# Choosing the gathered tokens first and the first tokens last in a two-block transformer kernel's expert layer

## The chip, the cores and the metric

The kernel runs on one core of one Trainium2 chip. The metric is the device time of one execution in microseconds (us). TensorE (PE in the rows) multiplies matrices, VectorE (DVE) and ScalarE (ACT) work element by element, GpSimd (POOL) does small element work here and issues the indirect DMAs, and SyncE (SP) issues most other DMAs. PEld is TensorE's loading of weights, which overlaps its matmuls.

## The reference

The program computes a first transformer block of two layers and then a second block; the change concerns only the end of the second block, a layer of 16,384 small experts for 512 tokens of 1024 values. Cut to that:

```python
def chunk_fn(hc):                                   # 128 tokens
    q = (hc @ w_query).reshape(128, 8, 256)         # 8 heads
    s1 = einsum('chk,nk->chn', q[..., :128], keys_1)
    s2 = einsum('chk,nk->chn', q[..., 128:], keys_2)
    v1, i1 = top_k(s1, 16)
    v2, i2 = top_k(s2, 16)
    cand = v1[..., :, None] + v2[..., None, :]      # 256 candidates per head
    top_s, pos = top_k(cand, 16)
    experts = take_along_axis(i1 * 128 + i2, pos)   # 16 experts per head
    gate = softmax(top_s)
    act = gelu(einsum('chkd,cd->chk', expert_u[experts], hc))
    return einsum('chk,chkd->cd', gate * act, expert_v[experts])
```

So each token has 8 x 16 = 128 chosen experts, each with a row of `expert_u` and a row of `expert_v` (1024 values each) and a gate.

## The kernel before

**Two ways for the experts.** The first 368 tokens (`TD`) are done densely: every expert's `u` is multiplied with all 368 tokens, GELU is taken, the result is multiplied with a gate that is zero where the expert was not chosen, and `v` is multiplied in. The last 144 tokens (`GTOK`) are gathered: for each of 144 columns one indirect DMA of 0.5 MB (`rows`, L1387) fetches one expert row for each of 128 tokens, VectorE multiplies it with the tokens' activations and sums (L1398), and after 144 rows of `u` come 144 rows of `v` (L1408). One such fetch with the vector instruction that belongs to it is called a gathered step here; there are 288, and step i works on the row that was fetched three steps earlier (`LAG`). Five `rows` tiles are there (`NROW`).

**fp32 by three products.** Each weight tile `raw` (1 MB) is split into a high part `whi` (ScalarE) and the rest `wlo` (VectorE), both at L242, and each product is three matmuls (`mm3`, L276 to L278). In the dense part a matmul has 368 columns. A unit is 1 MB of weights: two halves of 24 matmuls, 48 in all.

**The routing stage.** `w_query` gives the queries (matmuls of 512 columns), and for each head and chunk of 128 tokens `select(c, h)` takes the two top-16 lists and the top 16 of their sums on VectorE (L1170 to L1190, candidates added on GpSimd). `choose(c)` turns them into gates and row and column numbers of the experts (L1196 to L1236). `matrices(c)` transposes these on TensorE (L1263) and builds the gates of a dense chunk in slices of 16 tokens: for two steps per slice VectorE makes one-hot tiles `ob` (L1302) and `oa` (L1307, two of them), TensorE multiplies them (L1316, 32 matmuls of 128 columns in fp16 per slice), ScalarE copies the result (L1319) into `stage`, and a DMA puts it into DRAM (`gd`). Chunks 0, 1 and 2 have 8, 8 and 7 slices. Chunk 3 is gathered, as are the last 16 tokens of chunk 2.

**Order of the work.** `fill(n)` puts dense `u` units into this stage (12 in all, their results are written to DRAM as `spilled` and read back later by `back`); then come 8 more `up` units, and then the loop over 16 groups of 8 expert columns: the gates' tile `gt` (a DMA on ScalarE's queue, L1452), multiplication of `a` with it (L1464), a split of the product, 192 matmuls with `v`, and further `up` units. `pace()` advances the gathered steps evenly over this loop. A scheduler at build time puts each engine's instructions into one fixed order, with priorities given by `tc.high_priority`; it may put work of a later line ahead of an earlier one if tiles are free. Each engine then runs its own order strictly. A tile pool's memory goes to the next pool only after the pool is closed: `right` holds the routing stage's tiles `gm` and closes after the last `matrices`, and `er`, which comes after, takes the same memory.

In the kernel before, the chunks are chosen in the order 0, 1, 2, and 3 after `right.close()`; the tiles `a` that take the GELU results of all `u` units are in the pool `pp`, which is open from the start.

Of the kernel before, what the change touches and what calls it, by code (L numbers as in the profile page):

```python
# [21 lines left out]
P = 128  # L22
# [36 lines left out]
HNU = 4  # L59
# [10 lines left out]
OBB = 3  # L70
# [125 lines left out]
def block_kernel(ctx, tc, x_in, cs_in, wst, vec, cst, gmask, smask, pos, ada1, ada2, wgate, keys, ust, uex, vst, vex, out):  # L196
# [910 lines left out]
    with tc.tile_pool(name="peer", bufs=1, reuse_waits="tile") as pp:  # L1107
# [18 lines left out]
        def up(j2, eng=None, spill=None):  # L1126
            u = unit(ust[j2], eng=eng)
            for jj in range(2):
                p = bank("mm")
                for k in range(KD):  # L1130
                    o = (jj * KD + k) * P
                    mm3(p[:, :TD], *part(u, o, P), hh[k][:, :TD], hl[k][:, :TD],
                        k == 0, k == KD - 1)
                a = pp.tile([P, TD], F32, tag="a", bufs=NA, name="a")
                A_.activation(a, p[:, :TD], AF.Gelu_apprx_tanh)
                acts[2 * j2 + jj] = a
                if spill is not None:
                    SP.dma_start(spilled[spill + jj], a)

        def back(j2, spill):  # L1140
            for jj in range(2):
                a = pp.tile([P, TD], F32, tag="a", bufs=NA, name="a")
                SP.dma_start(a, spilled[spill + jj])
                acts[2 * j2 + jj] = a

        with tc.tile_pool(name="sel", bufs=1, reuse_waits="tile") as sp:
            cho = {}
# [100 lines left out]
            def matrices(c):  # L1248

                res = choose(c)  # L1250
                fill(FILL[c])
# [33 lines left out]
                for s in range(c0 // TS, min(c0 + P, TD) // TS):  # L1285
# [12 lines left out]
                    for q0 in range(0, 4, TQ):  # L1298
# [6 lines left out]
                        for i in range(2):  # L1305
                            o = gm.tile([P, TQ, P, 4], F16, tag=f"oa{i}", bufs=OBB, name="oa")
                            V.tensor_mul(  # L1307
# [4 lines left out]
                        for q in range(TQ):  # L1312
                            p = bank("acc")
                            for t in range(4):
                                for i in range(2):
# [6 lines left out]
                                 st.rearrange("p (g j) t -> p g j t", j=JG))  # L1322


            late = []
            for h in range(PH):
                qq, ql = [], []
                for half in range(2):
                    p = proj("w_query_2", hh, hl)
                    t = sp.tile([P, 3 * P], F32, tag="q", bufs=4, name="q")  # L1330
                    A_.copy(t, p[:, :S - P])
                    l = sp.tile([P, P], F32, name=f"ql{h}_{half}")
                    A_.copy(l, p[:, S - P:])
                    qq.append(t)
                    ql.append(l)
# [11 lines left out]
            if GTOK:  # L1347
                res = choose(NT - 1)
                V.tensor_copy(gates, res[0])
                V.scalar_tensor_tensor(eidx, res[1], 128.0, res[2], op0=ALU.mult, op1=ALU.add)  # L1350
            else:
                matrices(NT - 1)
# [6 lines left out]
        with tc.tile_pool(name="exp", bufs=1, reuse_waits="tile") as ep:  # L1359
            def gathered():  # L1360

                hn, hx = [er.tile([P, D], F32, name=f"hn{i}") for i in range(2)]
                with tc.high_priority(2 * AHEAD), tc.issue_after(mark.ins):
                    for e, tk in enumerate((slice(S - P, S), slice(TD, S - P))):
                        for k in range(KD):
                            if k % 4 == 0:
                                p = bank("acc")
                            t = er.tile([P, P], F32, tag="hs", bufs=2, name="hs")
                            if e:
                                V.tensor_add(t.rearrange("p (t q) -> p t q", q=EQ),  # L1370
                                             hh[k][:, tk, None].bitcast(F32).to_broadcast([P, EX, EQ]),
                                             hl[k][:, tk, None].bitcast(F32).to_broadcast([P, EX, EQ]))
                            else:
                                V.tensor_add(t, hh[k][:, tk].bitcast(F32), hl[k][:, tk].bitcast(F32))
                            T_.transpose(p[:, (k % 4) * P:(k % 4 + 1) * P], t, ident)
                            if k % 4 == 3:
                                A_.copy((hx if e else hn)[:, (k - 3) * P:(k + 1) * P], p)
                y, yx = [ep.tile([P, D], F32, name=f"y{i}") for i in range(2)]
                act = ep.tile([P, P + EX], F32, name="act")
                sel = ep.tile([P, EX], F32, name="sel")  # L1380
                V.reduce_sum(sel, ident.rearrange("p (t q) -> p t q", q=EQ), axis=mybir.AxisListType.X)
                rows = []
                for i in range(2 * (P + EX) + LAG):
                    if i < 2 * (P + EX):
                        n = i % (P + EX)
                        r = ep.tile([P, D], F32, tag="rows", bufs=NROW, name="rows")
                        G_.indirect_dma_start(out=r, out_offset=None, in_=uex if i < P + EX else vex,  # L1387
                                              in_offset=bass.IndirectOffsetOnAxis(
                                                  ap=eidx[:, n:n + 1] if n < P else eidx2[:, n - P:n - P + 1], axis=0))
                        rows.append(r)  # L1390
                    if i < LAG:
                        yield
                        continue
                    r = rows.pop(0)
                    n = (i - LAG) % (P + EX)
                    up_ = i - LAG < P + EX
                    if up_:
                        V.scalar_tensor_tensor(r, r, 1.0, hn if n < P else hx, op0=ALU.mult, op1=ALU.mult,  # L1398
                                               accum_out=act[:, n:n + 1])
                        if n == P + EX - 1:  # L1400
                            A_.activation(act, act, AF.Gelu_apprx_tanh)
                            V.tensor_mul(act[:, :P], act[:, :P], gates)
                            V.tensor_mul(act[:, P:], act[:, P:], gates2)
                    elif n in (0, P):
                        V.tensor_scalar(yx if n else y, r, act[:, n:n + 1], None, op0=ALU.mult)
                    else:
                        z = y if n < P else yx
                        V.scalar_tensor_tensor(z, r, act[:, n:n + 1], z, op0=ALU.mult, op1=ALU.add)  # L1408
                    yield
                for k in range(KD):  # L1410
                    if k % 4 == 0:
                        p = bank("mm")
                    T_.transpose(p[:, (k % 4) * P:(k % 4 + 1) * P], y[:, k * P:(k + 1) * P], ident)
# [165 lines left out]
```

## Time and profile before

| | |
|---|---|
| median of three runs | 2811.03 us (2804.39 to 2818.14) |
| the profiled execution's own time | 2807.13 us |
| its span, first to last instruction | 2805.4 us |
| TensorE busy | 2699.4 us, 96% |
| VectorE busy | 2095.0 us, 75% |
| matmuls | 14889 |
| mean granted TensorE clock | 0.988 of full |

A busy time adds the stretches in which an engine had an instruction in work; TensorE's matmuls overlap, so the time that one takes from its neighbours is read from the distance between two starts and not from the duration. The profile's line of slices cuts the span into 40 equal pieces of 70.1 us.

### The profile page before, as it was taken

Reading aid. Unit: us, or ns where it says so; the run is one execution under the profiler, and the core shown is the slowest. Engines: PE = TensorE matmul, PEld = TensorE weight load, DVE = VectorE, ACT = ScalarE, POOL = GpSimd, SP = SyncE. Lnnn points to the kernel's source line nnn. Section 1 sums busy time; section 2 is a strip of 40 time slices with the busy share of each in tenths; the row PEclk is TensorE's granted clock in tenths of the full one; section 3 lists DMA queues with packets and bytes.
Section 4 is the critical chain, followed back from the end, with each engine's and each line's share of the span. In section 5 each row is a group of like instructions: output and inputs, shape, how many; then the busy total and the mean of one; then the engine's idle time right before and its main releaser. Section 6 shows DMA issues by size and latency. Waiting matters only on the chain.

```text
span 2805.4 us, 38971 instructions
## 1 busy us (share of the span) xinstructions
PE 2699.4 (96%) x14889; PEld 2438.1 (87%) x14889; DVE 2095.0 (75%) x4028; ACT 1059.9 (38%) x1530; POOL 741.4 (26%) x638
## 2 busy tenths in 40 slices
PE   6789999999999999999999999999999999999998
PEld 4677888888788888888888789998999999999998
DVE  8874755556786654558866897789987988888996
ACT  4443422223443322233543246653333333333332
POOL 4631000000010100001511500004544545555550
PEclk9899999999999999999999999999999999999998
DMA  6441355553212555522222237667999998999983
GB/s 262 145 143 61 124 192 195 173 204 108 76 46 83 197 186 180 173 90 92 100 81 93 80 126 230 201 197 281 355 334 353 334 349 324 345 333 341 338 333 140
DMA packets 159788, 560.62 MB, mean 200 GB/s; under 512 B 13248, under 2 KB 66912, under 8 KB 124912
## 3 DMA queue, kind: packets, MB, share of 16 engines
q1 hardware_dynamic: 101648, 332.62, 33.7%
q0 software_dynamic: 55296, 201.35, 20.1%
q10 hardware_dynamic: 2656, 24.15, 2.2%
q8 instruction: 117, 1.92, 0.3%
q14 instruction: 71, 0.58, 0.1%
HBM read 527.32 MB, written 30.75 MB: 199 GB/s over the span
## 4 chain that ended last, share of the span: by engine, by line
PE 60%; DVE 14%; issue 12%; POOL 8%; DMA 5%; ACT 1%; POOLq 0%; SPq 0%; DVEq 0%; ACTq 0%
PE mm L277 15%; PE mm L276 15%; PE mm L278 15%; POOL rows L1387 7%; PE acc L1316 3%; DMA rows<-vex,eidx 3%; DVE wlo L242 3%; PE acc L278 2%; PE acc L277 2%; PE acc L276 2%; PE acc L646 1%; DMA rows<-uex,eidx 1%; PE acc L365 1%; DVE aw L481 1%; PE acc L935 1%
## 5 line engine op out<-in xcount | busy, mean ns | idle before, releaser
L242 ACT CAST whi<-raw 128x1024 fp32r<-128x1024 f32 x510 | 532.4, 1051 | 1304.3 <-PE mm L277 691.9
L277 PE MATMUL mm<-hl,whi 128*128 128x512 f32 (+2 forms) x2544 | 899.8, 354 | 4.0 <-DVE hl L429 3.1
L278 PE MATMUL mm<-hh,wlo 128*128 128x512 f32 (+2 forms) x2544 | 899.2, 354 | 3.6 <-DVE wlo L242 3.6
L276 PE MATMUL mm<-hh,whi 128*128 128x512 f32 (+2 forms) x2544 | 897.6, 354 | 4.2 <-ACT hh L428 3.2
L242 DVE TENSOR_TENSOR wlo<-raw,whi 128x1024 fp32r<-128x1024 f32 x488 | 598.9, 1231 | 234.6 <-ACT whi L242 223.6
L277 PEld LDWEIGHTS mm<-hl,whi 128*128 128x128 f32 x2544 | 482.3, 190 | 52.1 <-DVE hl L429 4.4
L278 PEld LDWEIGHTS mm<-hh,wlo 128*128 128x128 f32 x2544 | 482.7, 190 | 51.0 <-DVE wlo L242 4.4
L276 PEld LDWEIGHTS mm<-hh,whi 128*128 128x128 f32 x2544 | 481.1, 190 | 51.2 <-ACT hh L428 3.8
L1387 POOL DMA_INDIRECT rows<-vex,eidx x144 | 233.0, 1618 | 193.8 <-DVE y L1408 176.4
L1387 POOL DMA_INDIRECT rows<-uex,eidx x144 | 214.6, 1490 | 211.3 <-DVE rows L1398 165.8
L322 POOL DMA_DIRECT2D araw<-ada x96 | 51.0, 531 | 657.3 <-DVE araw L315 625.9
L1408 DVE SCALAR_TENSOR_TENSOR y<-rows,act,y 128x1024 f32<-128x1024 f32 x142 | 181.8, 1281 | 46.4 <-DMA rows<-vex,eidx 45.4
L1398 DVE SCALAR_TENSOR_TENSOR rows<-rows,hn 128x1024 f32<-128x1024 f32 x144 | 172.1, 1223 | 47.1 <-DMA rows<-uex,eidx 47.0
L315 DVE SCALAR_TENSOR_TENSOR araw<-araw,sc 128x1024 f32<-128x1024 f32 x128 | 158.1, 1258 | 8.7 <-DMA araw<-ada 8.7
L277 PE MATMUL mm<-fl,whi 128*128 128x512 f32 (+1 forms) x396 | 144.9, 366 | 0.0
L278 PE MATMUL mm<-fh,wlo 128*128 128x512 f32 (+1 forms) x396 | 144.9, 366 | 0.0
L276 PE MATMUL mm<-fh,whi 128*128 128x512 f32 (+1 forms) x396 | 144.7, 365 | 0.0
L743 DVE TENSOR_TENSOR s<-s,mm 128x512 f32<-128x512 f32 x42 | 28.9, 688 | 129.9 <-PE mm L278 129.4
L1319 ACT ACTIVATE stage<-acc 128x512 f32<-128x512 f32 x92 | 91.7, 1106 | 36.9 <-PE acc L1316 26.6
L451 DVE SCALAR_TENSOR_TENSOR x<-mm,mod,x 128x512 f32<-128x512 f32 (+1 forms) x66 | 44.1, 668 | 82.2 <-PE mm L278 82.1
L1316 PE MATMUL acc<-oa,ob 128*128 128x128 f16 x736 | 101.5, 296 | 0.3 <-DVE oa L1307 0.2
L1316 PEld LDWEIGHTS <-ob 128*128 128x128 f16 x736 | 76.8, 118 | 13.5 <-DVE oa L1307 0.6
(1383 smaller groups left out, 4659.9 us busy)
## 6 DMA issues: line engine op xcount, KB each, us to landing
raw<-wst SPq DMA_DIRECT2D x127, 1024.0 KB, 4.9
raw<-ust SPq DMA_DIRECT2D x64, 1024.0 KB, 7.1
raw<-vst SPq DMA_DIRECT2D x64, 1024.0 KB, 7.5
araw<-ada POOLq DMA_DIRECT2D x96, 512.0 KB, 4.5
gd<-stage SPq DMA_DIRECT2D x23, 1024.0 KB, 4.5
gt<-gd ACTq DMA_DIRECT2D x16, 1472.0 KB, 12.0
araw<-ada SPq DMA_DIRECT2D x32, 512.0 KB, 4.4
aw<-ada SPq DMA_DIRECT2D x16, 512.0 KB, 8.4
```

Of the source, the lines that this page charges most:

```text
L242: state["split"] = (A_.copy(hi, src), (eng or V).tensor_sub(lo, src, hi.bitcast(F32)))
L276: T_.matmul(out_, wh, ah, start=first, stop=False)
L277: T_.matmul(out_, wh, al, start=False, stop=False)
L278: state["mm"] = T_.matmul(out_, wl, ah, start=False, stop=last)
L315: op(out=w, in0=w, scalar=1.0, in1=sc, op0=ALU.mult, op1=ALU.mult, accum_out=out_)
L322: (G_ if l else SP).dma_start(raw, w[n * P:(n + 1) * P, :])
L451: return V.scalar_tensor_tensor(x[n][:, cs], p[:, cs], gate[:, n:n + 1], x[n][:, cs], op0=ALU.mult, op1=ALU.add)
L1316: T_.matmul(p[:, t * P:(t + 1) * P], ob[:, q, :, t], oa[i][:, q, :, t], start=i == 0, stop=i == 1)
L1319: A_.mul(st[:, :, t1:t1 + 4].rearrange("p j t -> p t j"), p.rearrange("p (t j) -> p t j", t=4), 1.0 / GSC)
L1387: G_.indirect_dma_start(out=r, out_offset=None, in_=uex if i < P + EX else vex, in_offset=bass.IndirectOffsetOnAxis(ap=eidx[:, n:n + 1] if ...
L1398: V.scalar_tensor_tensor(r, r, 1.0, hn if n < P else hx, op0=ALU.mult, op1=ALU.mult, accum_out=act[:, n:n + 1])
L1408: V.scalar_tensor_tensor(z, r, act[:, n:n + 1], z, op0=ALU.mult, op1=ALU.add)
```

## The change

The order of chunks in the routing stage is reversed. Chunk 3 is chosen first, right after the queries, and its gathered steps begin there: three at once, one after each slice of gates, and two after each of the eight `up` units. Then come `matrices(2)`, four heads of chunk 0's `select`, `matrices(1)`, the other four heads, and `matrices(0)`. The queries of chunk 0 are kept in the two tiles that later take `y` and `yx`. The tiles of the gathered part move to a pool `ga` that is open from before the routing stage. The tiles `a` are now a function `tile_a`: four of them in the routing stage's pool `sel`, for the units that are spilled, and after `right.close()` sixteen in `er`, in the memory that `gm` had. `ob` and `oa` have two buffers each where they had three (`OBB`). The first `gt` is allocated and loaded after the split weights' first tiles. Line numbers after the change are one lower up to L1102 and up to 72 and 19 higher behind (L1316 becomes L1388, L1398 becomes L1187, L1464 becomes L1483, L276 to L278 become L275 to L277).

```diff
-OBB = 3
+OBB = 2
...
+        ga = gs.enter_context(tc.tile_pool(name="ga", bufs=1, reuse_waits="tile"))
+        hn, hx = [ga.tile([P, D], F32, name=f"hn{i}") for i in range(2)]
+
+        def rows_tile():
+            return ga.tile([P, D], F32, tag="rows", bufs=NROW, name="rows")
...
+            def tile_a():
+                return sp.tile([P, TD], F32, tag="a", bufs=4, name="a")
...
-                a = pp.tile([P, TD], F32, tag="a", bufs=NA, name="a")
+                a = tile_a()
...
-                fill(FILL[c])
+                fill(FILL[NT - 2 - c])
...
                     SP.dma_start(gd[:, :, s, :, :].rearrange("g p j t -> p g j t"),
                                  st.rearrange("p (g j) t -> p g j t", j=JG))
+                    some(oh.ins)
...
-                for c in range(NT - 1):
-                    cs = slice(c * P, (c + 1) * P)
+                for c in (3, 2, 1):
+                    cs = slice((c - 1) * P, c * P)
                     select(c, h, qq[0][:, cs], qq[1][:, cs])
-                late.append(ql)
-            for c in range(NT - 1):
-                matrices(c)
+            res = choose(NT - 1)
+            V.tensor_copy(gates, res[0])
+            V.scalar_tensor_tensor(eidx, res[1], 128.0, res[2], op0=ALU.mult, op1=ALU.add)
+            side["g"] = gathered()
+            step(LAG)
+            done = [LAG]
+
+            def some(ins, n=1):
+                with tc.issue_after(ins):
+                    step(n)
+                done[0] += n
+
+            def late_select(hs):
+                for h in hs:
+                    select(0, h, late[0][:, h, :], late[1][:, h, :])
+
+            matrices(2)
+            late_select(range(0, 4))
+            matrices(1)
+            late_select(range(4, 8))
+            matrices(0)
             G_.memset(gm.tile([P, 120], F32, name="end"), 0.0)
             right.close()
-            er = ctx.enter_context(tc.tile_pool(name="er", bufs=1, side="right", reuse_waits="tile"))
-            for h in range(PH):
-                select(NT - 1, h, late[h][0], late[h][1])
...
             fill(NSP)
-            for j2 in range(NA // 2):
-                up(j2, eng=V)
-                if j2 == HNU:
-                    mark = state["mm"]
...
+        er = ctx.enter_context(tc.tile_pool(name="er", bufs=1, side="right", reuse_waits="tile"))
+
+        def tile_a():
+            return er.tile([P, TD], F32, tag="a", bufs=NA, name="a")
+
+        for j2 in range(NA // 2):
+            up(j2, eng=V)
+            some(state["split"][1].ins, 2)
...
-            per = (2.0 * (P + EX) + LAG - FIRST) / (todo - LAST)
-            step(FIRST)
+            per = (2.0 * (P + EX) + LAG - done[0]) / (todo - LAST)
...
-            gt = gate_load(0)
             for g in range(P // GJ):
...
+                    if j == 0:
+                        gt = gate_load(0)
```

The body of `gathered()` is the same but for its pool and for `y`, which is allocated at the first `v` row.

The order in which the instructions stand shows where the work went. First TensorE, at the place where the last dense chunk's gates begin. Before, this is chunk 2: the last gate matmuls (`acc<-oa,ob`) of chunk 1, one transpose of the gates `g`, and behind it matmuls of dense units (`mm<-hh,whi` and the like, 40 up to the next transpose).

```order
L1316 LDWEIGHTS ob
L1316 MATMUL acc<-oa,ob 128x128
L1263 MATMUL acc<-ct,g 128x128
L277 MATMUL mm<-hl_105,whi 128x368
L278 MATMUL mm<-hh_97,wlo 128x368
L276 MATMUL mm<-hh_98,whi 128x368
```

So the transposes had dense matmuls before and behind them. After the change the last dense chunk is chunk 0. Its place on TensorE reads as follows (`acc<-ky,ql` are the products of `select` for chunk 0).

```order
L1388 LDWEIGHTS ob
L1388 MATMUL acc<-oa,ob 128x128
L1237 MATMUL acc<-ky,ql 128x128 x5
L1335 MATMUL acc<-ct,g 128x128
L1335 MATMUL acc<-ct,e 128x128 x2
L1388 LDWEIGHTS ob
L1388 MATMUL acc<-oa,ob 128x128
```

No dense matmul stands there any more. In the order before, dense matmuls stand between the gate matmuls of every step of all three chunks. In the order after, 672 dense matmuls (14 units) stand ahead of chunk 1's first gate matmul, none between there and the last gate matmul of chunk 0 (512 gate matmuls), and 288 (6 units) in one block behind it.

The second place is VectorE where the gates are done and the dense groups begin. Before, the choosing of chunk 3 (`po`, `g`, `du`) stands between the multiplications with the gates' tile (`a<-a,gt`) and the splits:

```order
L1190 MAX_INDEX po<-top,w_15342 128x8
L242 TENSOR_TENSOR wlo<-raw,whi 128x1024
L1196 TENSOR_TENSOR g<-top 128x128
L1209 TENSOR_SCALAR du<-po 128x128 x2
L1464 TENSOR_TENSOR a<-a,gt 128x368 x3
L242 TENSOR_TENSOR wl__16336<-a,wh__16335 128x368
```

After, the last one-hot tiles of chunk 0 are followed by nine gathered steps, and then by the next split:

```order
L1374 TENSOR_TENSOR ob<-iot,cols 128x1024
L1379 TENSOR_TENSOR oa<-o_15290,o_15296 128x1024
L1379 TENSOR_TENSOR oa<-o_15291,o_15296 128x1024
L1187 SCALAR_TENSOR_TENSOR rows,act<-rows,hn_12117 128x1024 x9
L241 TENSOR_TENSOR wlo<-raw,whi 128x1024
L1483 TENSOR_TENSOR a<-a,gt 128x368 x5
```

Chunk 3's choosing is gone from there, and gathered steps have taken its place.

## Rows read from the trace of the kernel before

**Rows 1.** The page's head, its busy time by engine (share of the span, instructions), and TensorE's line of the 40 slices.

```profile
span 2805.4 us, 38971 instructions
PE 2699.4 (96%) x14889; PEld 2438.1 (87%) x14889; DVE 2095.0 (75%) x4028; ACT 1059.9 (38%) x1530; POOL 741.4 (26%) x638
PE   6789999999999999999999999999999999999998
```

**Rows 2.** Busy time by stretches of 70 us (columns: stretch, its length, then busy us and number of instructions of TensorE, its weight loads, VectorE, ScalarE, GpSimd, then granted TensorE clock, DMA share, GB/s): the gates, the change to the dense groups, and two stretches of the dense groups.

```profile
1750.00:1820.00 70.00, 69.94 (x493) 64.79 (x492) 54.28 (x105) 46.04 (x58) 0.00 (x0) 1.00 0.62 198
1890.00:1960.00 70.00, 63.02 (x358) 61.74 (x357) 63.11 (x149) 26.90 (x43) 29.14 (x23) 0.95 0.73 268
2100.00:2170.00 70.00, 68.42 (x407) 68.12 (x406) 57.56 (x89) 23.42 (x32) 36.68 (x24) 1.00 0.92 346
2170.00:2240.00 70.00, 70.00 (x420) 70.00 (x419) 61.46 (x96) 22.71 (x32) 35.92 (x24) 1.00 0.91 339
```

**Rows 3.** TensorE's instructions in order of time in a dense group (start, us, engine, line, instruction), the first and the last of 38 matmuls in a row.

```profile
2199.73 0.33 PE L278 MATMUL mm<-hh,wlo 128*128 128x368 f32 x1
...
2205.90 0.33 PE L276 MATMUL mm<-hh,whi 128*128 128x368 f32 x1
```

**Rows 4.** TensorE in order of time among the gates: sixteen gate matmuls, one dense matmul and the next gate matmuls.

```profile
1747.17 2.04 PE L1316 MATMUL acc<-oa,ob 128*128 128x128 f16 x16
1748.96 0.41 PE L277 MATMUL mm<-hl,whi 128*128 128x368 f32 x1
1749.21 0.53 PE L1316 MATMUL acc<-oa,ob 128*128 128x128 f16 x3
```

**Rows 5.** VectorE in order of time among the gates: the start of two steps, the first of the four instructions (`o`) that serve four slices, and the step behind them.

```profile
1757.41 0.68 DVE L1302 TENSOR_TENSOR ob<-iot,cols 128x1024 f16<-128x1024 f16 x1
...
1759.21 0.69 DVE L1302 TENSOR_TENSOR ob<-iot,cols 128x1024 f16<-128x1024 f16 x1
...
1761.02 0.42 DVE L1290 TENSOR_TENSOR o<-iot,dg 128x512 f16<-128x512 f16 x1
...
1762.63 0.69 DVE L1302 TENSOR_TENSOR ob<-iot,cols 128x1024 f16<-128x1024 f16 x1
```

**Rows 6.** VectorE in order of time in a dense group: a split and two gathered steps.

```profile
1970.42 1.22 DVE L242 TENSOR_TENSOR wlo<-raw,whi 128x1024 fp32r<-128x1024 f32 x1
1971.56 1.22 DVE L1398 SCALAR_TENSOR_TENSOR rows<-rows,hn 128x1024 f32<-128x1024 f32 x1
...
1972.70 1.22 DVE L1398 SCALAR_TENSOR_TENSOR rows<-rows,hn 128x1024 f32<-128x1024 f32 x1
```

**Rows 7.** VectorE in order of time in `select`: instructions of two of its top-16 rounds, each with its load of the compared values.

```profile
1888.06 0.07 DVE L1171 MATCH_VALUE_LOAD ii<-vv,acc 128x8 f32 x1
...
1888.32 0.07 DVE L1172 MATCH_VALUE_LOAD w<-vv,acc 128x8 f32 x1
...
1888.58 0.29 DVE L1170 MAX8 vv<-acc 128x8 f32<-128x128 f32 x1
1888.78 0.28 DVE L1173 MAX8 vv<-w 128x8 f32<-128x128 f32 x1
1888.98 0.08 DVE L1171 MATCH_VALUE_LOAD ii<-vv,acc 128x8 f32 x1
```

**Rows 8.** VectorE in order of time in `choose`: the first three additions, a comparison and a multiplication of one of its four pieces.

```profile
1655.22 0.42 DVE L1235 TENSOR_TENSOR eq<-eq 128x512 f16<-128x512 f16 x1
1655.55 0.69 DVE L1228 TENSOR_TENSOR eq<-io,rk 128x1024 f16<-128x1024 f16 x1
1656.16 0.28 DVE L1235 TENSOR_TENSOR eq<-eq 128x256 f16<-128x256 f16 x1
1656.36 0.69 DVE L1231 TENSOR_TENSOR eq<-eq,if__13143 128x1024 f16<-128x1024 f16 x1
```

**Rows 9.** ScalarE: in order of time the load of a function table ahead of `choose`'s exponential, and from the page's groups the copies of the gates (line, engine, operation, out<-in, count | busy us, mean ns of one | idle us before, what ended it).

```profile
1898.99 1.28 ACT L1197 ACT_TABLE_LOAD   x1
...
L1319 ACT ACTIVATE stage<-acc 128x512 f32<-128x512 f32 x92 | 91.7, 1106 | 36.9 <-PE acc L1316 26.6
```

**Rows 10.** Busy time by stretches of 10 us around the start of the dense groups (columns as in rows 2), and the longest wait of TensorE in 1890 to 1960 (engine, line, waited for, us, times, longest).

```profile
1890.00:1900.00 10.00, 6.98 (x41) 6.37 (x39) 10.00 (x43) 5.04 (x8) 2.11 (x4) 0.98 0.32 107
1900.00:1910.00 10.00, 7.07 (x26) 6.47 (x26) 10.00 (x33) 4.51 (x12) 0.00 (x0) 0.68 0.70 256
1910.00:1920.00 10.00, 8.97 (x53) 8.90 (x54) 9.34 (x23) 1.06 (x1) 4.23 (x3) 1.00 0.21 55
PE acc L277 <- DVE wl__16336 L242: 3.7, 1, 3.7
```

**Rows 11.** The same columns for three stretches of 10 us at the start of the program, where TensorE was partly idle.

```profile
90.00:100.00 10.00, 3.01 (x13) 3.04 (x14) 8.66 (x10) 1.11 (x5) 5.96 (x6) 0.52 0.65 213
110.00:120.00 10.00, 7.98 (x46) 7.01 (x45) 10.00 (x15) 2.44 (x4) 7.76 (x8) 0.89 0.58 171
140.00:150.00 10.00, 6.77 (x40) 5.16 (x40) 9.12 (x14) 4.67 (x8) 7.08 (x9) 1.00 0.60 200
```

**Rows 12.** From issue to landing: the gathered rows (shortest, median, longest), and from the page's DMA issues the gates' way out (`gd`) and back in (`gt`).

```profile
DMA to landing us min/median/max: 4.4/7.8/15.8
gd<-stage SPq DMA_DIRECT2D x23, 1024.0 KB, 4.5
gt<-gd ACTq DMA_DIRECT2D x16, 1472.0 KB, 12.0
```

More of the change, by code (lines that the diff above doesn't have):

```diff
@@ L1104, in block_kernel @@
     main.close()
-    with tc.tile_pool(name="peer", bufs=1, reuse_waits="tile") as pp:
+    with tc.tile_pool(name="peer", bufs=1, reuse_waits="tile") as pp, ExitStack() as gs:
         ky = pp.tile([P, 2, P], F32, name="ky")
@@ L1306, in matrices @@
                             o = gm.tile([P, TQ, P, 4], F16, tag=f"oa{i}", bufs=OBB, name="oa")
-                            V.tensor_mul(
+                            oh = V.tensor_mul(
                                 o.rearrange("p q (a b) t -> p q a b t", b=16),
@@ L1322, in matrices @@
                                  st.rearrange("p (g j) t -> p g j t", j=JG))
-            late = []
+                    some(oh.ins)
+            late = [ga.tile([P, PH, P], F32, tag=f"y{i}", name="ql") for i in range(2)]
             for h in range(PH):
-                qq, ql = [], []
+                t = rows_tile()
+                qq = []
                 for half in range(2):
                     p = proj("w_query_2", hh, hl)
[L1330 to L1335, printed above, removed]
-                for c in range(NT - 1):
-                    cs = slice(c * P, (c + 1) * P)
-                    select(c, h, qq[0][:, cs], qq[1][:, cs])
-                late.append(ql)
@@ L1340, in block_kernel @@
-            for c in range(NT - 1):
-                matrices(c)
+                    qq.append(t[:, half * S:half * S + S - P])
+                    A_.copy(qq[half], p[:, P:])
+                    A_.copy(late[half][:, h, :], p[:, :P])
+                for c in (3, 2, 1):
+                    cs = slice((c - 1) * P, c * P)
+                    select(c, h, qq[0][:, cs], qq[1][:, cs])
+            res = choose(NT - 1)
+            V.tensor_copy(gates, res[0])
+            V.scalar_tensor_tensor(eidx, res[1], 128.0, res[2], op0=ALU.mult, op1=ALU.add)
@@ L1342, in block_kernel @@
             G_.memset(gm.tile([P, 120], F32, name="end"), 0.0)
             right.close()
-            er = ctx.enter_context(tc.tile_pool(name="er", bufs=1, side="right", reuse_waits="tile"))
-            for h in range(PH):
-                select(NT - 1, h, late[h][0], late[h][1])
[L1347 to L1352, printed above, removed]
@@ L1353, in block_kernel @@
-            fill(NSP)
-            for j2 in range(NA // 2):
-                up(j2, eng=V)
-                if j2 == HNU:
-                    mark = state["mm"]
[L1359 to L1413, printed above, removed]
-                    gk = mods[2][:, 40 + k:41 + k]
-                    V.scalar_tensor_tensor(x[k][:, S - P:], p[:, (k % 4) * P:(k % 4 + 1) * P], gk, x[k][:, S - P:],
-                                           op0=ALU.mult, op1=ALU.add)
-                p = bank("mm")
-                for k in range(KD):
-                    gk = mods[2][:, 40 + k:41 + k]
-                    T_.matmul(p[:, k * EX:(k + 1) * EX], yx[:, k * P:(k + 1) * P], sel, start=True, stop=True)
-                    V.scalar_tensor_tensor(x[k][:, TD:S - P], p[:, k * EX:(k + 1) * EX], gk, x[k][:, TD:S - P],
-                                           op0=ALU.mult, op1=ALU.add)
-            side["g"] = gathered()
@@ L1449, in gate_load @@
             def gate_load(g):
-                gt = er.tile([P, 3072], F32, tag="gt", bufs=1, name="gt")[:, :TD * JG] \
+                gt = er.tile([P, 3064], F32, tag="gt", bufs=1, name="gt")[:, :TD * JG] \
                     .rearrange("p (s j t) -> p s j t", j=JG, t=TS)
```

66 lines of the change are left out of this document (64 added, 2 removed).

## The prediction

> **What bounds the kernel now.** I read the page first, then busy time by stretch for the last 1100 us, then the order of time on TensorE and VectorE where the change acts. The page says TensorE: 96% of the span, and nine tenths or more in nearly every slice [rows 1]. In the dense groups it has no free time to give: 38 matmuls of 368 columns start between 2199.73 and 2205.90, so one takes 6.17 / 37 = 0.167 us [rows 3], and 70 us hold 420 of them [rows 2]. The DMA engines are 91% busy there, but TensorE still starts a matmul every 0.167 us. The stretch where it does less, 2100 to 2170, has 407, that is 13 x 0.167 = 2.2 us lost [rows 2]. Among the gates it is busy 69.94 of 70 us while VectorE is busy 54 [rows 2], because dense matmuls stand between the gate matmuls. The one visible hole is at the start of the dense groups: 1890 to 1920 hold 41 + 26 + 53 = 120 matmuls, 20.0 us of work in 30, so 10 us are lost; TensorE waits up to 3.7 us for VectorE, which is busy 10.00 of 10 with choosing chunk 3, and the granted clock of 1900 to 1910 is 0.68, so part of that stretch ran at the lower level [rows 10].
>
> So the reader should ask of each edit what it does to TensorE's supply of work. An engine that is bound gains nothing from lighter DMA traffic beside it.
>
> **The change part by part.** TensorE's work is the same: the same matmuls in another order. What counts is where it waits.
>
> *The hole in chunks 1 and 0.* This is the largest term. The `a` tiles of the eight later units now lie in the memory that the gates' tiles hold until chunk 0 is done. The four PSUM banks `mm` take two of these units without an `a` tile, so the order has 12 + 2 = 14 units ahead and then nothing dense until the last gate matmul. Between, TensorE runs at VectorE's speed.
>
> VectorE's time there, by distances between starts: one step (`ob` and two `oa`) 1759.21 - 1757.41 = 1.80 us, and an `o` group 1762.63 - 1761.02 = 1.61 [rows 5]; a gathered step 1.14 [rows 6]. In `select` a find or a replacement with its load takes 0.26 and a maximum 0.20 [rows 7]; a round has two maxima, two finds and one replacement, 1.18, and a select three rounds (two lists, one list of sums), 3.5. In `choose` a piece has a comparison 0.61, a multiplication 0.60 (taken as the comparison's neighbour, same shape), additions of 0.33, 0.20 and about 0.13, and a last one of about 0.14: 2.0 us [rows 8]; four pieces 8.0, and a dozen small ones about 0.2 each, 2.4. Chunks 1 and 0 have 16 slices: 32 steps 57.6, four `o` groups 6.4, 16 gathered steps 18.2, four selects 14.0, one choose 10.4, small table preparation 2.0: 108.6 us. Of that 3.7 (two `ob`, an `o` group, the smallest ones) lie ahead of chunk 1's first `oa`, under dense matmuls; 105 remain. Where select and choose have nothing beside them, hand-overs show: the products that select waits for, GpSimd's candidates, the exponential with its table load of 1.28 [rows 9], the transposes and ScalarE's three copies. No row has them bare; I take 6 us (3 to 12). TensorE's last step adds 2. Stretch: 113 us.
>
> TensorE's work in it: sixteen gate matmuls take 1748.96 - 1747.17 = 1.79, 0.112 each [rows 4]; 512 take 57.3, transposes and products 2: 59. **Hole: 113 - 59 = 54 us** (48 to 60). ScalarE's four copies to a slice, 4 x 1.106 = 4.4 us [rows 9], stay below VectorE's 3.6 + 0.4 + 1.14 = 5.2 and are not the limit.
>
> Some comes back: a dense matmul behind gate matmuls takes 1749.21 - 1748.96 = 0.25 instead of 0.167 [rows 4], and some 58 such changes disappear: **-5**.
>
> *Ahead of that.* Choosing chunk 3 first gives VectorE 10.4 for choose, 16 additions of 0.2 for the activations, and four more splits of 1.14 [rows 6]: 18 us more ahead of the first gate matmul; the order gives 322 - 221 = 101 more dense matmuls there as cover, 16.8 us. **0** (0 to 6). Chunk 2's slices stay covered: 7 slices need 7 x 5.2 = 36 on VectorE and some eight splits 9, against 25 of gate and 26 of dense matmuls (153); with two `ob` buffers instead of three VectorE is two steps ahead, which is enough as long as it isn't the slower one. Then four selects, choose and nine splits (14 + 10 + 10, preparation 3) stand against 197 dense matmuls, 33 us: **+5** (0 to 8).
>
> *Behind it.* Six units follow; two are split already, 96 matmuls, 16 us. VectorE does nine gathered steps first. About five rows are in when it comes there; each further one needs a free tile, an issue and a landing of 7.8 [rows 12], so it is busy for some 14 us. The first GELU results must wait for the gates' memory, and `gt` comes 4.5 + 12.0 after the last slice [rows 12], by which time some 16 us of dense matmuls have run. **+4** (0 to 12; at the upper end a late row holds up the split behind it). TensorE restarts twice after a pause; between 1900 and 1910 matmuls stood 0.27 us apart, not 0.167 [rows 10]. **+3** for that.
>
> *What is gained.* The 10 us at the start of the dense groups go, since choosing chunk 3 no longer competes with the first gate products: **-10** (-10 to 0). Later, 42 of 291 steps are already done, so the pace per unit falls from 287/106 = 2.71 to 249/106 = 2.35 steps. If every matmul missing from 420 per 70 us was lost to that, as in the stretch with 407, it would be about 8 us over eleven stretches; **-3** (-8 to 0).
>
> *Sum:* 54 - 5 + 0 + 5 + 4 + 3 - 10 - 3 = +48. The profiled execution took 2807.13, its span 2805.4; with 48 it gives 2855. The three runs' median is 3.9 above that execution, so 2859 by the median; I say 2857. Lower ends of all terms: 48 - 5 + 0 + 0 + 0 + 0 - 10 - 8 = +25, 2832. Upper ends, with the clock as in the first rival: 60 - 5 + 6 + 8 + 12 + 29 = +110, 2917; not all of these come together, so 2900.
>
> **The rivals.**
>
> *Half clock in the hole (0.15).* If TensorE ran chunks 1 and 0 at its lower level (1.2 GHz instead of 2.4), a gate matmul would take nearly 0.112 x 0.27 / 0.167 = 0.18 to 0.22 us, 32 of them 5.8 to 7.2, more than VectorE's 5.2 per slice; taking 6.8, 16 x 1.6 = +26, near 2883. For it: 3.01 us busy of 10 came with a granted clock of 0.52. Against it: 6.77 and 7.98 of 10 came with 1.00 and 0.89 [rows 11], and here the share is 3.6 of 5.2, 0.69. The Trainium skill ("TensorE: Matmul & The Clock Gate", Part 1: The HAM clock gate) says that the throttled state is the default and that activity releases it; by that rule chunks 1 and 0 could fall to half rate as a whole, and the sum would be that of this rival. The traced stretches between speak for the full level, so I keep it as the rival.
>
> *A new stall where the old one was (0.15).* Nine gathered steps, a `gt` that comes late and `a` tiles that wait for the gates' memory hold VectorE and ScalarE while six units need splits. If the 10 us come back and the upper end of 12 holds: 48 + 10 + 8 = +66, 2875. It decides once VectorE reaches the split behind the nine steps later than about 20 us after its last `oa`.
>
> *Faster (0.03).* The dense groups may be held by the 0.91 DMA share after all. Then lighter gathering gives the 8 us there, and with the 10 us at their start 18: 2811 - 18 = 2793. That needs the hole to be nearly nothing, VectorE's 105 us to shrink towards TensorE's 59. It decides from a hole below 18 us, a VectorE stretch of 77; no row points there.
>
> *No change (0.05).* Gains at their ends (-23 with the switches) and a hole of half the size, if VectorE runs well ahead in chunk 2 and so covers chunk 1: about 2811 to 2822.
>
> **How the numbers follow.** My forecast has 0.62 (2835 to 2872). Half a per cent, 14 us, is about what a measurement of this kernel can tell from no change. Slower by more: 0.62 + 0.15 + 0.15 = 0.92; within: 0.05; faster: 0.03. The range 2830 to 2900 leaves out the two last cases and the worst of the first two.
>
> **What would show it.** Right: in the trace after, some 110 us between chunk 1's first gate matmul and chunk 0's last in which VectorE is busy nearly throughout and TensorE about half, an idle piece of some 30 us in one (choosing chunk 0), no stall of 3.7 us for `wl` at the first dense group, and dense groups still at 415 to 420 matmuls per 70 us. Wrong: gate matmuls over 0.15 us apart in that stretch (first rival), waits for gathered rows or `gt` behind it (second), or clearly more matmuls per 70 us in the dense groups (third). The sum fails if the built order isn't what limits TensorE.

## The result and the profile after

The changed kernel takes 2842.9 us (median of four runs, 2840.73 to 2844.06); the kernel before, beside it, 2807.7 (2804.37 to 2818.14). The ratio is 1.0126, 95% interval 1.0104 to 1.0147: 35 us slower. Forecast were 2857 and a range of 2830 to 2900. The span grew from 2805.4 to 2841.6, 36.2 us.

The page of the changed kernel: head, busy time, and the 40 slices of TensorE and of its granted clock.

```profile
span 2841.6 us, 38968 instructions
PE 2699.1 (95%) x14889; PEld 2440.7 (86%) x14889; DVE 2104.2 (74%) x4028; ACT 1073.7 (38%) x1530; POOL 707.1 (25%) x638
PE   6789999999999999999999999679999999999998
PEclk9899999999999999999999999669999999999998
```

TensorE's busy time is that of before [rows 1]. What is new stands in two slices, 6 and 7: the hole; the granted clock falls beside it. Busy time by 10 us (us, then PE, weight loads, VectorE, ScalarE, GpSimd with instructions; granted clock, DMA share, GB/s):

```profile
1800.00:1810.00 10.00, 7.03 (x56) 6.12 (x55) 10.00 (x19) 8.03 (x9) 2.08 (x2) 0.67 1.04 324
...
1840.00:1850.00 10.00, 0.95 (x2) 0.36 (x2) 9.66 (x40) 1.20 (x5) 0.66 (x2) 0.50 0.00 1
1850.00:1860.00 10.00, 1.02 (x5) 0.67 (x6) 8.73 (x26) 0.71 (x3) 0.00 (x0) 0.50 0.00 0
...
1900.00:1910.00 10.00, 8.13 (x36) 8.13 (x36) 4.17 (x8) 4.32 (x8) 6.03 (x6) 0.67 1.00 334
1910.00:1920.00 10.00, 10.00 (x62) 10.00 (x61) 6.11 (x11) 1.96 (x4) 2.62 (x2) 1.00 0.94 390
```

VectorE is full or nearly so while TensorE has seven to nine tenths of work among the gates (1800 to 1810 is at the low end) and a tenth while chunk 0 is chosen. The order of time on TensorE (start, us, instruction, count, idle time ahead and what ended it) shows the edges:

```profile
1787.36 0.40 PE L1388 MATMUL acc<-oa,ob 128*128 128x128 f16 x2 [3.66 <-DVE oa L1379]
...
1843.77 0.47 PE L1335 MATMUL acc<-ct,g 128*128 128x128 f32 x1 [12.27 <-DVE g L1273]
1849.19 0.48 PE L1335 MATMUL acc<-ct,e 128*128 128x128 f32 x1 [4.95 <-DVE e L1308]
1853.22 0.47 PE L1335 MATMUL acc<-ct,e 128*128 128x128 f32 x1 [3.55 <-DVE e L1308]
1859.24 0.40 PE L1388 MATMUL acc<-oa,ob 128*128 128x128 f16 x2 [5.55 <-DVE oa L1379]
...
1894.22 3.70 PE L1388 MATMUL acc<-oa,ob 128*128 128x128 f16 x30 [0.19 <-DVE oa L1379]
1901.87 0.68 PE L275 MATMUL mm<-hh,whi 128*128 128x368 f32 x1 [3.95 <-ACT a L1134]
```

From chunk 1's first gate matmul to chunk 0's last: 1894.22 + 3.70 - 1787.36 = 110.6 us. VectorE's order there gives the period of a slice: its gathered steps (one instruction each) are 4.76 us apart, which is two steps of 1.80 and one gathered step of 1.14, as forecast from [rows 5, 6].

```profile
1860.91 1.22 DVE L1187 SCALAR_TENSOR_TENSOR rows<-rows,hn 128x1024 f32<-128x1024 f32 x1
1865.67 1.22 DVE L1187 SCALAR_TENSOR_TENSOR rows<-rows,hn 128x1024 f32<-128x1024 f32 x1
1870.43 1.22 DVE L1187 SCALAR_TENSOR_TENSOR rows<-rows,hn 128x1024 f32<-128x1024 f32 x1
```

In the dense groups the answer to [rows 2] is

```profile
2170.00:2240.00 70.00, 70.00 (x422) 70.00 (x421) 60.67 (x95) 26.92 (x38) 28.40 (x21) 1.00 0.89 319
```

and every 70-us window from 1960 to 2730 has 422 matmuls. Before, these eleven windows held 4574, now 4642: 68 x 0.167 = 11.3 us gained. My 420 was not full: a window also counts the matmuls that reach over its edges, two more, so full is 70 / 0.1667 + 2 = 422.

### The profile page after: what moved, and what is told of

Its sections match the earlier page's. It is cut to its first block, busy times and chain, and to the rows that moved or that the text cites. A ratio compares the mean times of both kernels' runs of the same rounds, so it can differ in the third digit from the quotient of the medians.

```text
span 2841.6 us, 38968 instructions
## 1 busy us (share of the span) xinstructions
PE 2699.1 (95%) x14889; PEld 2440.7 (86%) x14889; DVE 2104.2 (74%) x4028; ACT 1073.7 (38%) x1530; POOL 707.1 (25%) x638
## 4 chain that ended last, share of the span: by engine, by line
PE 82%; DVE 12%; ACT 2%; DMA 1%; issue 1%; POOL 1%; SPq 0%; DVEq 0%; ACTq 0%; POOLq 0%
PE mm L276 19%; PE mm L275 19%; PE mm L277 18%; PE acc L276 6%; PE acc L275 6%; PE acc L277 6%; DVE wlo L241 2%; PE acc L1388 1%; DVE aw L480 1%; PE acc L645 1%; PE acc L364 1%; DVE oa L1379 1%; PE acc L934 1%; ACT stage L1391 1%; DVE ii L1246 1%
## 5 line engine op out<-in xcount | busy, mean ns | idle before, releaser
L275 PE MATMUL mm<-hh,whi 128*128 128x512 f32 (+2 forms) x2544 | 897.7, 354 | 7.8 <-ACT a L1134 4.0
L276 PE MATMUL mm<-hl,whi 128*128 128x512 f32 (+2 forms) x2544 | 899.9, 354 | 4.0 <-DVE hl L428 3.1
L277 PE MATMUL mm<-hh,wlo 128*128 128x512 f32 (+2 forms) x2544 | 899.2, 354 | 0.0
L275 PEld LDWEIGHTS mm<-hh,whi 128*128 128x128 f32 x2544 | 481.6, 190 | 54.6 <-ACT a L1134 4.2
L276 PEld LDWEIGHTS mm<-hl,whi 128*128 128x128 f32 x2544 | 482.5, 190 | 52.3 <-DVE hl L428 4.4
L277 PEld LDWEIGHTS mm<-hh,wlo 128*128 128x128 f32 x2544 | 482.9, 190 | 47.7 <-issue 1.5
L1176 POOL DMA_INDIRECT rows<-uex,eidx x144 | 196.0, 1361 | 380.7 <-DVE rows L1187 356.4
L1176 POOL DMA_INDIRECT rows<-vex,eidx x144 | 217.4, 1509 | 272.9 <-DVE y L1199 241.8
L1187 DVE SCALAR_TENSOR_TENSOR rows<-rows,hn 128x1024 f32<-128x1024 f32 x144 | 171.6, 1219 | 7.8 <-DMA rows<-uex,eidx 7.8
L276 PE MATMUL mm<-fl,whi 128*128 128x512 f32 (+1 forms) x396 | 145.1, 367 | 0.0
L277 PE MATMUL mm<-fh,wlo 128*128 128x512 f32 (+1 forms) x396 | 145.1, 366 | 0.0
L275 PE MATMUL mm<-fh,whi 128*128 128x512 f32 (+1 forms) x396 | 144.9, 366 | 0.0
L1388 PE MATMUL acc<-oa,ob 128*128 128x128 f16 x736 | 96.5, 297 | 22.0 <-DVE oa L1379 18.1
L1388 PEld LDWEIGHTS <-ob 128*128 128x128 f16 x736 | 81.9, 121 | 33.0 <-issue 14.2
```

The costliest lines, as they stand in the source:

```text
L275: T_.matmul(out_, wh, ah, start=first, stop=False)
L276: T_.matmul(out_, wh, al, start=False, stop=False)
L277: state["mm"] = T_.matmul(out_, wl, ah, start=False, stop=last)
L1388: T_.matmul(p[:, t * P:(t + 1) * P], ob[:, q, :, t], oa[i][:, q, :, t], start=i == 0, stop=i == 1)
```

## The experiments

There are two questions: whether the hole is VectorE's pace with nothing else for TensorE in the order; and where 11.3 us in the dense groups came from, when I had 3. For the second, the distances between the `v` products' matmuls spoke for the part of the change that I had priced at nothing, `gt` behind `wh_` and `wl_` (the tiles of the split products that the `v` matmuls stream).

**Placement, alone and undone.** All ratios are to the kernel before.

> The changed kernel with the gates' tile gt ahead of wh_ and wl_ again, as in the kernel before, and its 3072 elements; nothing else differs. In the built programs wh_ and wl_ then start 32 bytes off a multiple of 64 (byte 204768), as before the change; in the changed kernel they start on one (192512). Theory P (this placement makes the matmuls of the v products slower): those matmuls stand 0.1688 us apart again instead of 0.1667; 3072 of them by 0.0021 give 6.6 us, so near 2849.5 us, 1.0149 of the kernel before, and fewer than 422 matmuls in the 70-us windows of the dense groups. Theory G (the gain there came from fewer gathered steps per unit): no change, 2843 us, 0.1667 and 422.

```diff
+            gt = gate_load(0)
             for g in range(P // GJ):
...
-                    if j == 0:
-                        gt = gate_load(0)
```

(and 3072 for 3064). Measured: 2849.3, 1.0152 (1.0129 to 1.0176). Ninety-six `v` matmuls, first and last, of the changed kernel and then of this one:

```profile
2016.17 0.33 PE L275 MATMUL acc<-wh__17025,whi 128*128 128x368 f32 x1
...
2032.00 0.33 PE L277 MATMUL acc<-wh__17060,wlo 128*128 128x368 f32 x1
```

```profile
2016.95 0.33 PE L275 MATMUL acc<-wh__17025,whi 128*128 128x368 f32 x1
...
2032.99 0.33 PE L277 MATMUL acc<-wh__17060,wlo 128*128 128x368 f32 x1
```

15.83 / 95 = 0.1666 against 16.04 / 95 = 0.1688, with TensorE busy without a break in both, and this kernel's windows have 418 to 420. Theory P: 3072 matmuls by 0.0022 are 6.7 us, and the medians are 6.4 apart. The spacing is the evidence; the two ratios' intervals overlap.

> The kernel before with one part of the change alone: gt is taken behind the first wh_ and wl_, with 3064 elements, so that wh_ and wl_ start at byte 192512, a multiple of 64. Theory P: the v products' matmuls stand 0.1667 us apart instead of 0.1688, 6.6 us less, near 2801 us, 0.9977 of the kernel before. Theory G: no difference, 1.000, and 0.1688 as before.

```diff
-            gt = gate_load(0)
             for g in range(P // GJ):
...
+                    if j == 0:
+                        gt = gate_load(0)
```

Measured: 2804.2, 0.9994 (0.9979 to 1.0008), no difference. Yet its `v` matmuls stand at (2016.28 - 2000.44) / 95 = 0.1667:

```profile
2000.44 0.33 PE L276 MATMUL acc<-wh__16944,whi 128*128 128x368 f32 x1
...
2016.28 0.33 PE L278 MATMUL acc<-wh__16979,wlo 128*128 128x368 f32 x1
```

So P holds for the pace and fails for the time. Two of its windows, and what VectorE waits for from 1960 to 2730 (us, times, longest):

```profile
2030.00:2100.00 70.00, 70.00 (x422) 70.00 (x421) 63.99 (x99) 24.41 (x34) 40.39 (x26) 1.00 0.94 348
...
2170.00:2240.00 70.00, 68.20 (x407) 67.90 (x408) 61.59 (x96) 23.06 (x35) 35.99 (x24) 1.00 0.88 321
```

```profile
DVE y L1408 <- DMA rows<-vex,eidx: 45.0, 13, 6.6
DVE rows L1398 <- DMA rows<-uex,eidx: 43.0, 18, 5.6
```

VectorE waits 88 us for gathered rows, the splits behind it come late (TensorE waits 6.8 us for `wlo`), and TensorE loses 9.7 of 770 us. The kernel before has the same waits:

```profile
DVE y L1408 <- DMA rows<-vex,eidx: 45.4, 13, 5.9
DVE rows L1398 <- DMA rows<-uex,eidx: 40.9, 15, 5.6
```

The changed one has only

```profile
DVE rows L1187 <- DMA rows<-uex,eidx: 0.9, 1, 0.9
```

To see whether the gathering takes what the placement gives, two kernels leave out 42 of the 291 steps (and with them a part of the last 144 tokens' result):

> The kernel before with gt behind wh_ and wl_ and 3064 elements, and with 21 of the 144 gathered columns left out of u and of v (so 42 of 291 steps, and their part of the last 144 tokens' result); pace 249 instead of 291 steps over the loop, as in the changed kernel. Without the lighter gathering this kernel lost 9.7 us of 770 to waits in the dense groups. Theory W (the gathered steps hold TensorE up there, and the placement of wh_ and wl_ pays only when they don't): windows of 422 and 70.00, 10 us less than with all steps, near 2794, 0.9955 of the kernel before. Rival (the waits come from where the loads of u and v stand, not from the number of steps): windows of 400 to 422 as with all steps, 2804.

> The kernel before with 42 of the 291 gathered steps left out (21 of 144 columns of u and of v, and their part of the last 144 tokens' result), gt ahead of wh_ and wl_ as before, so these 32 bytes off a multiple of 64. Theory: no waits of VectorE for rows in the dense groups (the kernel before had 86 us of them), windows full with 70.00, but at 0.1688 us for the v products 418 to 420 matmuls, not 422: 6.5 us more than with gt behind (2800.4), near 2807 and so no faster than with all steps. Rival (lighter gathering alone brings the gain): 2800, as with gt behind.

```diff
+COLS = [n for n in range(P + 16) if not 100 <= n < 121]
...
-                for i in range(2 * (P + EX) + LAG):
+                for i in range(2 * M + LAG):
...
-                        n = i % (P + EX)
+                        n = COLS[i % M]
```

Measured: with `gt` behind 2800.4, 0.9981 (0.9969 to 0.9993); with `gt` ahead 2808.6, 0.9995 (0.9983 to 1.0008). In both VectorE waits 1.0 us for rows and TensorE is busy 770.00 of 770; the windows have 421 to 422 and 418 to 419:

```profile
2170.00:2240.00 70.00, 70.00 (x422) 70.00 (x421) 56.03 (x85) 26.27 (x36) 30.78 (x21) 1.00 0.89 315
```

```profile
2170.00:2240.00 70.00, 70.00 (x419) 70.00 (x418) 56.72 (x86) 24.48 (x33) 27.61 (x21) 1.00 0.87 314
```

So each part alone gives nothing that can be told from noise, and both together 5 us, 0.2%, with an interval that just leaves 1 out. I expected 10: the dense groups do give 11 (4641 matmuls), but at their start a new wait of 5.1 us for `wlo` stands beside the old 3.7.

**The hole.**

> The changed kernel without the one gathered step after each slice of gates; these 23 steps go into the dense groups, whose pace rises from 2.35 to 2.57 steps per unit. Theory V (VectorE's 4.75 us per slice set the pace of chunks 1 and 0): 16 x 1.14 = 18 us off the stretch, 110.5 becomes 92 and the time 2825. Theory A (ScalarE's four copies of 1.106 = 4.42 us per slice come next): only 16 x 0.33 = 5 us, stretch 105, time near 2838, and TensorE's waits in the slices then name the copies to stage. In both the dense groups stay at 422 matmuls per 70 us unless 2.57 steps per unit are already too many; a missing 8 us there would show as windows of 414 to 418.

```diff
-                    some(oh.ins)
```

Measured: 2824.6, 1.0063 (1.0048 to 1.0078). The profiled execution, with 2831.0 the longest of six, shows:

```profile
1782.30 0.40 PE L1388 MATMUL acc<-oa,ob 128*128 128x128 f16 x2 [0.74 <-DVE oa L1379]
...
1854.18 15.36 PE L1388 MATMUL acc<-oa,ob 128*128 128x128 f16 x126 [0.21 <-DVE oa L1379]
...
1882.61 3.83 PE L1388 MATMUL acc<-oa,ob 128*128 128x128 f16 x31 [0.60 <-ACT stage L1391]
1889.91 0.68 PE L275 MATMUL mm<-hh,whi 128*128 128x368 f32 x1 [3.47 <-ACT a L1134]
```

The stretch is 104.1 us, theory A's 105: without the step, ScalarE's copies and TensorE's own 32 matmuls ((15.36 - 0.30) / 125 = 0.120 each) are the next limits. So the gathered steps account for 6.5 us of the stretch and not for the 18 of their own time. That the time fell by 18, as V says, is no proof of V: 5 us come from chunk 1 starting earlier (1782.30, not 1787.36), which fits chunk 2's seven steps that VectorE no longer has ahead of it, and 6 us are the distance of this execution to its median, which stays unplaced.

> The changed kernel with all eight selects of chunk 0 between the gates of chunks 2 and 1. VectorE's work from chunk 2 to chunk 0 is the same, and it is busy throughout: theory V says that TensorE's idle piece at choosing chunk 0 shrinks by the four selects' 14 us while chunk 1's gates start 14 us later, so the time is that of the changed kernel, 2843, within 5 us either way. Rival (the piece in which chunk 0 is chosen is a loss by itself, with its hand-overs): 10 to 14 us faster, near 2830.

```diff
-            late_select(range(0, 4))
+            late_select(range(0, 8))
             matrices(1)
-            late_select(range(4, 8))
```

Measured: 2834.2, 1.0096 (1.0081 to 1.0111), 8.7 us faster than the changed kernel, between the two. VectorE idles 1.8 us from 1760 to 1890, where the changed kernel's idles 5.7 from 1760 to 1900: of these 4 us, 2.3 are waits of `select` for its products and 1.0 a split's wait for ScalarE. The rest isn't placed.

> The changed kernel with 16 instead of 12 u units whose results are written out and read back: the built order then has 192 more dense matmuls between the gate matmuls of chunk 1, none between those of chunk 0 or while chunk 0 is chosen. Theory F (TensorE stood idle for want of work in the order, and VectorE's own time sets the stretch): 192 x 0.167 = 32 us of TensorE's work move into idle time, VectorE gets eight splits of 1.14 = 9 us there: about -23, near 2820 us, and the stretch from chunk 1's first gate matmul to chunk 0's last grows from 110.5 to about 120. Rival (what is added there delays the gates by as much as it saves, since VectorE is full and a split late by some us holds TensorE up): the stretch grows by some 32 and the time stays near 2843.

> The changed kernel with 20 instead of 12 units written out: the built order has 192 more dense matmuls in chunk 1's gates and another 191 while chunk 0 is chosen. Theory F: 384 x 0.167 = 64 us of TensorE's work find 52 us of idle time, VectorE's 105 us become 105 + 16 x 1.14 = 123 and with hand-overs 131: the stretch grows by some 20 and the work behind shrinks by 64, less some 3 us of changes between shapes: -41, near 2802 us. Rival as with 16: the time stays near 2843; or, if reading back 16 more tiles holds up the dense groups, those show waits for a.

```diff
-NSP = 12
+NSP = 20
```

Measured: 2832.4, 1.0092 (1.0072 to 1.0112) with 16, and 2806.5, 1.0004 (0.999 to 1.0017) with 20. The first is half of theory F's gain, the second 36 of its 41 us. TensorE's order with 16 units:

```profile
1866.84 0.48 PE L1335 MATMUL acc<-ct,g 128*128 128x128 f32 x1 [15.86 <-DVE g L1273]
...
1926.17 0.68 PE L275 MATMUL mm<-hh,whi 128*128 128x368 f32 x1 [5.17 <-ACT a L1134]
```

and the span of its gate matmuls (count, ns, first and last start), after that of the changed kernel:

```profile
L1388 PE MATMUL acc<-oa,ob x736: 275/298/315, 1694.5 to 1897.6; 128*128 128x128 f16 x184
```

```profile
L1388 PE MATMUL acc<-oa,ob x736: 275/297/303, 1696.5 to 1920.7; 128*128 128x128 f16 x184
```

The gates end 23 us later, for 32 us of work moved. Idle time can't be pooled: chunk 1's gates have some 8 x (4.76 - 32 x 0.117) = 8 us of it, and 32 us of dense work there make TensorE the limit (busy 59.95 of 60 us from 1790), VectorE wait (13 us for splits, where it waited 1), and choosing chunk 0 begin later with its whole idle piece (15.86, 4.95, 3.55, 5.55 us of waits) still ahead. The next four units stand in that piece, fill it, and give the 26 us.

**The hole filled.**

> The changed kernel with 24 units written out. Against 20, another 192 dense matmuls stand in chunk 0's gates, which with 20 units still had 13 us of idle time on TensorE in 38 us; the pace is 2.65 steps per unit. Theory F: 32 us of work move, of which 13 us fill idle time, and the rest makes chunk 0 wait for TensorE as chunk 1 does with 16: -13 against 2806.5, so near 2794, 0.9955 of the kernel before. Rival (the dense groups, now with 2.65 steps per unit and 24 more tiles to read back, lose it): windows below 420 there and 2800 to 2807.

> As with 24 units, and gathered steps only after chunk 2's slices: 16 steps go from chunks 1 and 0 into the dense groups, pace 2.82 per unit, more than the 2.71 of the kernel before. With TensorE the limit in chunks 1 and 0 by then, VectorE's 18 us there should give little: theory W says that the dense groups lose by the pace what the kernel before lost to it, some 8 us, so 2800 to 2806 and slower than the version with steps after every slice; the rival (VectorE's steps still set chunks 1 and 0) says 10 to 15 us faster than that version.

> The changed kernel with 24 units written out and gathered steps only after the slices of chunks 2 and 1, pace 2.73 per unit. Against 24 units with steps after every slice: no steps hold up the last slices, so the stall of some 5 us ahead of the first dense group goes, and 8 more steps fall into the dense groups. If these take them without VectorE waiting over 20 us for rows there: near 2787, 0.993 of the kernel before; otherwise 2792 as the two versions on either side.

> The kernel before with gt behind wh_ and wl_ (3064 elements) and 24 instead of 12 units written out, without the reversed order. Theory O (the order of the chunks and the early gathered steps are needed for the gain of the 24 units): TensorE has no hole among the gates here that the units could fill, and the gathered steps crowd into fewer units behind, 287/94 = 3.05 per unit: VectorE waits for rows as much as before or more, 2804 us or above. Rival S (units written out early gain by themselves): near 2792 as with the reversed order.

```diff
-NSP = 12
+NSP = 24
...
-                    some(oh.ins)
+                    if c:
+                        some(oh.ins)
```

(in the third; `if c == NT - 2` in the second). Measured: 2791.7, 0.9942 (0.9926 to 0.9957); 2791.6, 0.9952 (0.9934 to 0.997); 2789.2, 0.9934 (0.9918 to 0.995); and without the reversed order 2829.7, 1.0077 (1.006 to 1.0093). The third's TensorE slices show no hole:

```profile
PE   6789999999999999999999999999999999999998
```

So the first three are faster than both kernels, by 0.5 to 0.7% of before. The first is near theory F's 2794. The third waits 28 us for rows, more than its condition of 20, and lies between its two forecasts. Theory O holds for the time: 24 units in the old order make it slower. Its reason doesn't: VectorE waits 51 us for rows there, less than the 86 of before, and TensorE's longest sum of waits is 19.7 us for VectorE's `x`. Whether the early gathered steps or the order of the chunks is what the 24 units need was not tested apart. In the dense groups TensorE is busy 741 of 770 us:

```profile
2310.00:2380.00 70.00, 65.36 (x385) 63.86 (x385) 65.43 (x105) 25.03 (x38) 33.24 (x26) 1.00 0.94 353
```

In the second kernel theory W missed, and its rival too: the time is that of the first. At 2.82 steps per unit, more than before's 2.71, VectorE waits 22 us for rows and TensorE loses 0.8 of 770. So the number of steps per unit doesn't decide by itself. What else keeps the kernel before behind at 2.71 stays open; its weights also come late (ScalarE waits 326 us for `raw` from 1960 to 2730, in the second kernel 39).

## Why the prediction was right, and its terms

- **The hole**, 54, and -5 for changes between shapes: right in mechanism and, in part by luck, in size. The stretch is 110.6 for 113, with VectorE's period per slice as forecast, and the waits while chunk 0 is chosen are 12.27, 4.95, 3.55 and 5.55, 26 us (forecast some 30). The experiments that filled it gave the time back: 51 us from 12 to 24 units. But a gate matmul takes 0.117 us and not 0.112. I had taken the start of the next dense matmul for the end of sixteen; by their own starts they stand (2.04 - 0.30) / 15 = 0.116 apart [rows 4]. So TensorE's work is 62 and the hole 110.6 - 62 = 49. The -5 goes with it: sixteen gate matmuls and a dense one take 1749.21 - 1747.17 = 2.04 there, and 16 x 0.117 + 0.167 is 2.04, so that change between shapes costs nothing that shows. The two errors cancel.
- **Ahead of it**, 0 and +5: the first gate matmul starts at 1694.5 instead of 1675.1, 19.4 us for 16.8 of dense work, +3; ahead of chunk 1 TensorE waits 3.66 and some 0.9: +5 as forecast, though this leaves out what TensorE had lost at the like place before (from 1675.1 to 1890, 215 us, it ran 736 gate and 704 dense matmuls, 86 + 117 = 203 us of work, and 54 small ones).
- **Behind it**, +4 and +3: the wait for the GELU result is 3.95 us, as much as forecast, but ScalarE shows no wait for the gates' memory. Its last copies end at 1900.03, a function table loads for 1.28, and GELU follows at once:

```profile
1896.21 3.82 ACT L1391 ACTIVATE stage<-acc 128x512 f32<-128x512 f32 x4 [1.19 <-DMA gd<-stage]
1900.05 1.28 ACT L1134 ACT_TABLE_LOAD   x1
1901.34 1.59 ACT L1134 ACTIVATE a<-mm 128x368 f32<-128x368 f32 x4
```

  So the number came by luck. The dense matmuls then start at the lower level; 36 matmuls in the 8.13 us from 1901.87 to 1910, where 0.167 would give some 49, cost 2.
- **The old stall**, -10: gone. No wait ahead of the first dense group besides the 3.95.
- **Dense groups**, -3 (-8 to 0): mis-sized, -11.3. Its bound rested on 420 as full, and the edit of `gt`, at nothing, had no term. The undone placement costs 6.4; the rest, some 5, is the waits (3.8 of 770 us by TensorE's busy sum before, none after) and the rounding of the counts. So the forecast's sentence that a bound engine gains nothing from lighter DMA traffic beside it doesn't hold here: 42 gathered steps less took away the 9.7 us that TensorE lost in the kernel before with `gt` behind.
- Sum with what was measured: 49 + 0 + 3 + 5 + 4 + 2 - 10 - 11 = 42, against 36 in the span; 6 us stay unplaced, and the loss that the +5 leaves out is of that kind. The forecast stood 14 us too high: 8 from the dense groups, 2 from its choice of 2857 over 2855, and 4 that are the unplaced 6 less 2 by which the other terms were too low.
- **Rival one** (half clock): its condition came in part, its price didn't. The granted clock in the gates changed between its two levels, 0.50 and 1.00, with means of 0.67 over 10 us, where I had trusted the rows with 0.89 and 1.00 [rows 11]. But a gate matmul takes (3.70 - 0.30) / 29 = 0.117 us, not 0.18 to 0.22, and as many start at either level. Within the run of 126 gate matmuls of the kernel without the steps (TensorE alone, columns as before):

```profile
1855.00:1859.00 4.00, 4.00 (x36) 0.50 0.02 4
1861.00:1865.00 4.00, 4.00 (x36) 1.00 0.91 276
```

  I had scaled it like a dense matmul, which does slow down (0.306 us at 1902 to 1906, at the lower level). The Trainium skill ("TensorE: Matmul & The Clock Gate", Part 1: The HAM clock gate) gives 55.6 ns for 128 columns at the full level and 106.7 at the lower. The 0.117 comes near the second and not near the first, at either level, so something other than the clock holds these matmuls at the full level; what it is was not tested, and the measurement decides.
- **Rival two** (a new stall): it didn't come. VectorE reaches the split behind the nine steps at 1913.36, 17 us after its last `oa`, and TensorE doesn't wait for it; the 3.95 is ScalarE's.

```profile
1913.36 1.22 DVE L241 TENSOR_TENSOR wlo<-raw,whi 128x1024 fp32r<-128x1024 f32 x1
```

- **Rival three** (faster): dense groups gave its 8 us and more, but the hole stayed; with it filled, the time comes near its 2793.

## What to carry to other kernels

What it gives to fill an idle piece of the limiting engine depends on where in the order the added work stands. Dense work added among chunk 1's gates, where TensorE was nearly busy, delayed VectorE's chain by 23 of the 32 us that it moved; added where TensorE waits for that chain, it gave back 26 of 32. The order that costs 1.3% gained up to 0.7% once it had enough independent units for the hole it made. And two edits that each measured nothing gained 0.2% together: lighter gathering (which leaves out part of the result) took away the waits that hid the gain of the placement.

## What had not been expected of the hardware

A matmul of 368 columns of fp32 stands 0.1688 us from the next where its moving operand starts 32 bytes off a multiple of 64 in its partition (byte 204768), and 0.1667 where it starts on one (byte 192512): 1.3%. The kernel before, its version with lighter gathering and the changed kernel with `gt` ahead are of the first kind; the changed kernel and the two of before with `gt` behind, with all steps and with fewer, are of the second. Only these two places were tried, so that the offset from 64 is what counts is not shown. And the gate matmuls (128 columns of fp16, both operands read at every fourth element) took 0.117 us at the full granted clock and at half of it.
